# A matmul with a decaying cumulative sum: the second quarter of w as float32 by SyncE's queue

## The chip, the cores and the metric

The kernel runs on one core of a Trainium2 chip. The metric is the device time of one execution in microseconds (us). Three runs of the kernel before gave 904.08, 904.32 and 904.46 us, median 904.32. Engines are called as in the profile: PE (TensorE, matmuls), PEld (its weight loads), DVE (VectorE), ACT (ScalarE), POOL (GpSimd) and SP (SyncE, which only issues transfers).

## The reference

```python
B, S, D = (16, 2048, 1024)      # x [B,S,D], w [D,D], decay [D], all float32

def reference(x, w, decay):
    xw = x @ w
    out[:, 0, :] = xw[:, 0, :]
    for t in range(1, S):
        out[:, t, :] = decay * out[:, t - 1, :] + xw[:, t, :]
    return out
```

A matrix product, and along time a first-order recurrence for each of the 1024 output columns.

## The kernel before

Time is cut into 64 chunks of 512 steps (`chunks`, four for each of the 16 batches). The 1024 input columns are cut into four quadrants of 256, each on 32 partitions. x is loaded by POOL's queue and cast to bfloat16 on the way (`load`, line 105), turned in blocks of 32 by 32 on DVE (`turn`, line 115, tile `xw`), and copied apart into `xt` (`part`, line 123), the form in which the matmuls read it. In the first two chunks some matmuls read `xw` directly.

Eight matmuls, k = 0 to 7, sum over the input columns; k = 2m + e, with m the row set (0 to 3) and e the parity of the row of w. Eight output groups n = 0 to 7 of 128 columns belong to two halves h of w's columns. So w comes in four quarters (h, e), each of four row sets m. A quarter is loaded into `stage[h, e]`, which borrows room from output tiles (`room`), by four transfers, one for each quadrant (`load_w`, line 319). It is then settled into the weight tile `wsb`, row set by row set, by a copy on DVE or ACT that also makes it bfloat16 if it isn't (`settle`, line 326; `settle_slots`, line 375, does one row set in two pieces).

- Quarter (0,0) comes as float32, two transfers by SP's queue and two by ACT's, at the very start.
- Quarters (0,1), (1,0), (1,1) are issued by POOL, cast to bfloat16 during the transfer.

The first four output groups run together for the first two chunks (step 0 of the main loop): first all even k of chunk 0, in two half chunks (columns of time 0 to 255, then 256 to 511), then k = 1, 3, 5, 7 of chunk 0 for four groups each, then chunk 1. So quarter (0,0) and x's first half chunk are needed first, then the second half chunk, then quarter (0,1), row set after row set, then chunk 1. Quarters (1,0) and (1,1) are needed from the fifth output group on.

Nothing is scheduled by a planner: every instruction is kept in the order of the program on its engine, and `agenda` is a list of steps written out by hand, each a letter and a number. The entry -99 is the order of the start:

- `M0` to `M3`: loads of x's half chunks (chunk 0 first half, second half, chunk 1 first half, second half), four transfers each by POOL.
- `U0` to `U2`: `load_part`, the last three quarters of w by POOL.
- `w0 W1 w2 W3`: settle quarter (0,0); small `w` on ACT, `W` on DVE. `q4 w5 Q4 W6 W7` settle quarter (0,1): `q4` and `Q4` are row set 0 in two pieces on DVE, `w5` row set 1 on ACT, `W6` and `W7` row sets 2 and 3 on DVE. `W8` to `W11` and `w12` to `w15` settle the last two.
- `K0` to `K3`: `spin_on`, ACT copies one column of quadrant q of x's first half chunk into a gate tile, on which a few idle matmuls wait.
- `E0` to `E15`: turns on DVE, four for each half chunk; `F` and `G`: the copies into `xt` on DVE and ACT.
- `D`: the decay rows are turned, copied and squared on DVE.

POOL's queue holds eight transfers before an issue has to wait for the one eight places earlier to land.

After the start the kernel repeats: matmuls for two chunks and one output group, the recurrence on DVE and, for some tiles, in pairs with POOL and ACT, turning back on DVE, stores by SP's queue (`Outlet.store`, line 302).

Of the kernel before, what the change touches and what calls it, by code (L numbers as in the profile page):

```python
# [10 lines left out]
BF16 = mybir.dt.bfloat16  # L11
# [3 lines left out]
def _ap(ap_obj: bass.AP, new_ap, extra_offset=0):  # L15
    return dataclasses.replace(
        ap_obj,
        ap=[list(p) for p in new_ap],
        offset=ap_obj.offset + extra_offset,
    )  # L20
# [5 lines left out]
def kernel(  # L26
# [26 lines left out]
    nc = tc.nc  # L53
    pin = tc.keep_in_program_order
    B, S, D = x.shape
    assert w.shape == (D, D)

    NQ = 4
    P = 32
    CQ = D // NQ  # L60
    K = CQ // P
    M = K // 2
# [4 lines left out]
    CH = D // 2  # L67
# [8 lines left out]
    def ring(pool, name, count, shape, dtype=FP32):  # L76
        i = turns[name] = turns.get(name, -1) + 1
        return pool.tile(shape, dtype, name=f"{name}{i % count}")

    def quad(q):  # L80
        return slice(q * P, (q + 1) * P)
# [12 lines left out]
    def ot_tile(nj):  # L94
        return ring(sb, "ot", 4, [128, nj, CR])

    xb_of = {}
# [12 lines left out]
    def turn(c, j0=0, j1=NJ, m0=0, m1=M):  # L110
        if c not in xw_of:
            xw_of[c] = ring(sb, "xw", 2, [128, M, NJ, P, 2], BF16)
        src = xb_of[c][:, j0:j1].rearrange("p j c -> p (j c)").bitcast(FP32)
        dst = xw_of[c].rearrange("p m j i e -> p (m j i e)").bitcast(FP32)
        pin(nc.vector.transpose(  # L115
            out=dst.rearrange("p (m j i) -> p j m i", m=M, i=P)[:, j0:j1, m0:m1],
            in_=src.rearrange("p (j m c) -> p j m c", m=M, c=P)[:, :, m0:m1]))
# [168 lines left out]
    class Outlet:  # L286
# [8 lines left out]
        def store(self, b, t0):  # L295
# [4 lines left out]
            for j in range(0, self.nj, nj):  # L300
# [9 lines left out]
    room = [ot_tile(2 * NJ).rearrange("p j c -> p (j c)") for _ in range(2)]  # L310
    size = M * CH
    stage = {(0, 0): room[0][:, 0:size],
             (0, 1): room[0][:, size:size * 3 // 2].bitcast(BF16),
             (1, 0): room[1][:, 0:size // 2].bitcast(BF16),
             (1, 1): room[1][:, size // 2:size].bitcast(BF16)}

    def load_w(queues, h, e):
        for i, q in enumerate((0, 2, 1, 3)):
            pin(queues[i % len(queues)].dma_start(  # L319
                out=stage[h, e][quad(q)].rearrange("p (m d) -> p m d", m=M),  # L320
                in_=_ap(w, [[2 * D, P], [2 * P * D, M], [1, CH]],
                        (q * CQ + e) * D + h * CH)))
# [26 lines left out]
    for q in range(NQ):  # L349
        pin(nc.sync.dma_start(  # L350
            out=rows[q * P:q * P + R],
            in_=_ap(decay, [[P, R], [CH, 2], [1, P]], q * CR)))
# [8 lines left out]
        spin(3 if q < NQ - 1 else 2, gates[q])  # L361

    def load_part(i):
        load_w((nc.gpsimd,), *((0, 1), (1, 0), (1, 1))[i])

    def part_one(i, copy):
        part(i // 8, copy, i % 4, i % 4 + 1, *halves[i // 4 % 2])
# [105 lines left out]
    def turn_and_load(c):  # L473
# [16 lines left out]
        "w": lambda i: settle_one(i, nc.scalar.copy),  # L490
        "M": load_half,
        "U": load_part,
        "E": lambda i: turn(i // 8, *halves[i // 4 % 2], i % 4, i % 4 + 1),
        "F": lambda i: part_one(i, nc.vector.tensor_copy),
        "G": lambda i: part_one(i, nc.scalar.copy),
# [22 lines left out]
        "L": lambda i: load(*loads.pop(0)) if loads else None,  # L518
    }
    agenda = {  # L520
        -99: "M0 M1 U0 M2 M3 U1 U2 w0 W1 w2 W3 K0 K1 K2 K3 E0 E1 G0 E2 G1 E3 F2 G3 E4 E5 G4 E6 G5 E7 F6 G7 q4 w5 Q4 W6 W7 D E8 E9 G8 E10 G9 E11 F10 G11 E12 L E13 G12 L E14 G13 E15 L F14 G15",
        0: "p0 z0 W8 W9 W10 W11",
        1: "g0",
        2: "L S1 L",
# [199 lines left out]
```

## Time and profile before

| | |
|---|---|
| median of three runs | 904.32 us (904.08 to 904.46) |
| the profiled execution, its own time | 903.77 us |
| its span | 902.0 us |
| POOL's queue (q0): packets, MB, share of 16 engines | 137024, 68.70, 56.9% |
| SP's queue (q1): packets, MB, share of 16 engines | 265808, 134.77, 60.6% |
| w by POOL's queue | 12 transfers of 128 KB, 5.1 us median from issue to landing |
| w by SP's and ACT's queues | 2 + 2 transfers of 256 KB, 4.7 and 5.2 us |
| x half chunks | 16 transfers of 128 KB, 5.9 us |

The span runs from the first to the last recorded instruction; the execution's own time is a little longer. Sizes are those written into the core's memory: a quarter of w is 1 MB as float32 and 512 KB as bfloat16. Where a matmul or a copy sat idle, the timeline names in brackets for how long and what ended the wait. A wait for several transfers ends with the last of them.

### The profile page before, as it was taken

Reading aid. Unit: us, or ns where it says so; the run is one execution under the profiler, and the core shown is the slowest. Engines: PE = TensorE matmul, PEld = TensorE weight load, DVE = VectorE, ACT = ScalarE, POOL = GpSimd, SP = SyncE. Lnnn points to the kernel's source line nnn. Section 1 sums busy time; section 2 is a strip of 40 time slices with the busy share of each in tenths; the row PEclk is TensorE's granted clock in tenths of the full one; section 3 lists DMA queues with packets and bytes.
Section 4 is the critical chain, followed back from the end, with each engine's and each line's share of the span. In section 5 each row is a group of like instructions: output and inputs, shape, how many; then the busy total and the mean of one; then the engine's idle time right before and its main releaser. Section 6 shows DMA issues by size and latency. Waiting matters only on the chain.

```text
span 902.0 us, 12224 instructions
## 1 busy us (share of the span) xinstructions
PE 892.4 (99%) x4127; PEld 412.1 (46%) x4209; DVE 824.9 (91%) x635; ACT 687.6 (76%) x962; POOL 656.6 (73%) x755
## 2 busy tenths in 40 slices
PE   9999999999999999999999999999999999999998
PEld 5544444444444444444444444444444444444444
DVE  4999998999999999999998999999999999999998
ACT  4889967777877877878778778777787787787743
POOL 7888678777767778777677686777777777776532
PEclk9999999999999999999999999999999999999999
DMA  9999999999999999999999999999999999999858
GB/s 191 194 215 220 229 243 218 215 218 249 244 243 254 231 258 251 251 243 250 225 234 227 223 234 224 232 228 226 233 230 227 227 231 225 226 228 222 176 146 239
DMA packets 403182, 204.77 MB, mean 227 GB/s; under 512 B 9392, under 2 KB 402096, under 8 KB 403120
## 3 DMA queue, kind: packets, MB, share of 16 engines
q1 hardware_dynamic: 265808, 134.77, 60.6%
q0 software_dynamic: 137024, 68.70, 56.9%
q8 instruction: 33, 0.54, 0.2%
q10 hardware_dynamic: 288, 0.52, 0.2%
q14 instruction: 29, 0.24, 0.1%
HBM read 138.42 MB, written 134.22 MB: 302 GB/s over the span
## 4 chain that ended last, share of the span: by engine, by line
PE 97%; DMA 1%; issue 1%; POOL 0%; DVE 0%; ACT 0%; DVEq 0%; POOLq 0%
PE ps L131 96%; PE spare L131 1%; DMA xb<-in_x_dram 1%; DMA ot<-in_w_dram 1%; POOL ot L319 0%; DVE so L233 0%; POOL xb L105 0%; PE ps L415 0%; PE spare L415 0%; ACT xb L422 0%; DVE wsb L375 0%; DVEq L375 0%; POOLq L708 0%
## 5 line engine op out<-in xcount | busy, mean ns | idle before, releaser
L131 PE MATMUL ps<-xt,wsb 128*128 128x512 bf16 x3934 | 860.8, 378 | 4.5 <-DVE wsb L375 0.2
L131 PEld LDWEIGHTS <-wsb 128*128 128x128 bf16 x4160 | 406.7, 98 | 478.7 <-ACT wsb L326 0.8
L208 POOL TENSOR_TENSOR xs<-h,xs 128x512 f32<-128x512 f32 (+1 forms) x190 | 242.8, 1278 | 188.2 <-ACT h L169 85.0
L186 ACT COPY xs<-ps 128x1024 f32<-128x1024 f32 (+1 forms) x190 | 188.8, 994 | 153.6 <-PE ps L131 143.2
L278 DVE STREAM_TRANSPOSE ot<-so 128x1024 f32<-128x1024 f32 (+2 forms) x264 | 300.2, 1175 | 2.3 <-POOL so L202 1.1
L266 POOL TENSOR_TENSOR so<-h,xs 128x512 f32<-128x512 f32 (+1 forms) x190 | 241.1, 1271 | 42.6 <-ACT h L169 27.1
L123 ACT COPY xt<-xw 128x2048 bf16<-128x2048 bf16 (+1 forms) x136 | 242.3, 1790 | 7.8 <-DVE xw L115 7.8
L105 POOL DMA_DIRECT2D xb<-in_x_dram x264 | 173.9, 660 | 3.4 <-DMA ot<-in_w_dram 1.3
L169 ACT ACTIVATE h<-so,dec 128x512 f32<-128x512 f32 (+1 forms) x190 | 145.5, 766 | 27.8 <-DVE so L213 24.5
L115 DVE STREAM_TRANSPOSE xw<-xb 128x2048 f32<-128x2048 f32 (+1 forms) x78 | 147.3, 1901 | 6.7 <-DMA xb<-in_x_dram 6.7
L213 DVE TENSOR_TENSOR_SCAN so<-spare,keep,xs 128x512 f32<-128x512 f32 (+1 forms) x97 | 119.9, 1239 | 26.7 <-POOL xs L208 26.3
L213 DVE TENSOR_TENSOR_SCAN so<-spare,xs 128x512 f32<-128x512 f32 x93 | 113.3, 1220 | 27.2 <-POOL xs L208 24.4
L169 ACT ACTIVATE h<-ps,dec 128x512 f32<-128x512 f32 (+1 forms) x189 | 129.5, 685 | 0.0
L233 DVE TENSOR_TENSOR_SCAN so<-dec,ps 128x1024 f32<-128x1024 f32 x34 | 76.9, 2260 | 0.8 <-ACT h L169 0.6
L233 DVE TENSOR_TENSOR_SCAN so<-dec,keep,ps 128x1024 f32<-128x1024 f32 (+2 forms) x35 | 74.7, 2137 | 0.0
L270 ACT COPY keep<-so 128x1 f32<-128x1 f32 x136 | 25.2, 188 | 9.2 <-DVE so L233 8.7
L204 ACT COPY so<-keep 128x1 f32<-128x1 f32 x97 | 18.4, 191 | 2.5 <-DVE ot L278 2.3
L131 PE MATMUL spare<-xt,wsb 128*128 128x512 bf16 (+1 forms) x64 | 12.9, 332 | 0.0
L131 PE MATMUL ps<-xw,wsb 128*128 128x256 bf16 (+1 forms) x68 | 11.2, 301 | 0.0
L202 POOL MEMSET so<- 128x1 f32 x93 | 10.7, 117 | 0.6 <-DVE ot L278 0.6
L319 POOL DMA_DIRECT2D ot<-in_w_dram x12 | 6.5, 545 | 3.6 <-DMA xb<-in_x_dram 2.5
L344 PE MATMUL spare<-idle 128*128 128x512 bf16 x22 | 7.1, 499 | 1.2 <-DVE idle L334 1.2
(40 smaller groups left out, 40.5 us busy)
## 6 DMA issues: line engine op xcount, KB each, us to landing
out_dram<-ot SPq DMA_DIRECT2D x236, 512.0 KB, 11.1
xb<-in_x_dram POOLq DMA_DIRECT2D x248, 256.0 KB, 7.9
out_dram<-ot SPq DMA_DIRECT2D x56, 128.0 KB, 2.6
xb<-in_x_dram POOLq DMA_DIRECT2D x16, 128.0 KB, 5.9
out_dram<-ot SPq DMA_DIRECT2D x8, 256.0 KB, 4.5
ot<-in_w_dram POOLq DMA_DIRECT2D x12, 128.0 KB, 5.1
out_dram<-xb SPq DMA_DIRECT2D x4, 256.0 KB
ot<-in_w_dram ACTq DMA_DIRECT2D x2, 256.0 KB, 5.2
```

Source lines behind the costliest of these rows:

```text
L105: pin(nc.gpsimd.dma_start(out=xb_of[c][quad(q), j0:j1], in_=_ap(x, [[D, P], [P * D, j1 - j0], [1, CQ]], (b * S + t0 + j0 * P) * D + q * CQ)))
L115: pin(nc.vector.transpose(out=dst.rearrange("p (m j i) -> p j m i", m=M, i=P)[:, j0:j1, m0:m1], in_=src.rearrange("p (j m c) -> p j m c", ...
L123: pin(copy(out=xt_of[c][:, m0:m1, :, j0 * P:j1 * P], in_=src))
L131: pin(nc.tensor.matmul(out=ps[:, t0:t1] if ps.shape[1] >= t1 else ps, lhsT=lhs, rhs=rhs, start=(k == 0 and t0 == start), stop=(k == K - 1),))
L169: pin(nc.scalar.activation(out=h, in_=src, func=mybir.ActivationFunctionType.Copy, scale=dec[:, self.n:self.n + 1]))
L186: pin(nc.scalar.copy(out=self.xs[:, i * size:(i + 1) * size], in_=ps))
L208: pin(nc.gpsimd.tensor_tensor(out=odds, in0=self.g, in1=odds, op=ALU.add))
L213: pin(nc.vector.tensor_tensor_scan(out=so[:, 3:T + 2:2], data0=squares[-1][:, n:n + 1].to_broadcast([128, T // 2]), data1=self.xs[:, 1:T:2 ...
L233: pin(nc.vector.tensor_tensor_scan(out=so[:, t + 2:t + 2 + size], data0=dec[:, n:n + 1].to_broadcast([128, size]), data1=ps, initial=befor ...
L266: pin(nc.gpsimd.tensor_tensor(out=self.so[:, 2:T + 2:2], in0=self.h, in1=self.xs[:, 0:T:2], op=ALU.add))
L270: pin(nc.scalar.copy(out=self.keep, in_=self.so[:, self.T + 1:self.T + 2]))
L278: pin(nc.vector.transpose(out=outlet.ot[:, :, c0:c0 + P], in_=self.so[:, 2 + t0:2 + t0 + nj * P].rearrange("p (i t) -> p i t", t=P)))
```

## The change

The second quarter of w, (0,1), is no longer cast in the transfer. Its place in `stage` is twice as long and holds float32. `U0` is gone, and `load_part` now serves the last two quarters only. A new step `O` (`load_rows`) stands behind the gate copies K0 to K3: ACT copies one element of the last quadrant of x's first half chunk into the stage, and then SP issues eight transfers of 128 KB: row sets 0 and 1 of all four quadrants, then row sets 2 and 3. The first transfer overwrites the copied element and so waits for the copy; the other seven stand behind it in SP's queue.

```diff
     stage = {(0, 0): room[0][:, 0:size],
-             (0, 1): room[0][:, size:size * 3 // 2].bitcast(BF16),
+             (0, 1): room[0][:, size:2 * size],
              (1, 0): room[1][:, 0:size // 2].bitcast(BF16),
              (1, 1): room[1][:, size // 2:size].bitcast(BF16)}
...
     def load_part(i):
-        load_w((nc.gpsimd,), *((0, 1), (1, 0), (1, 1))[i])
+        load_w((nc.gpsimd,), 1, i - 1)
+
+    def load_rows(i):
+        pin(nc.scalar.copy(
+            out=stage[0, 1][quad(0), 0:1], in_=xb_of[0][quad(NQ - 1), 0, 0:1]))
+        for m in range(0, M, 2):
+            for q in range(NQ):
+                pin(nc.sync.dma_start(
+                    out=stage[0, 1][quad(q), m * CH:(m + 2) * CH].rearrange(
+                        "p (m d) -> p m d", m=2),
+                    in_=_ap(w, [[2 * D, P], [2 * P * D, 2], [1, CH]],
+                            (q * CQ + 2 * m * P + 1) * D)))
...
+        "O": load_rows,
...
-        -99: "M0 M1 U0 M2 M3 U1 U2 w0 W1 w2 W3 K0 K1 K2 K3 E0 E1 G0 E2 G1 E3 F2 G3 E4 E5 G4 E6 G5 E7 F6 G7 q4 w5 Q4 W6 W7 D E8 E9 G8 E10 G9 E11 F10 G11 E12 L E13 G12 L E14 G13 E15 L F14 G15",
+        -99: "M0 M1 M2 M3 U1 U2 w0 W1 w2 W3 K0 K1 K2 K3 O E0 E1 G0 E2 G1 E3 F2 G3 E4 E5 G4 E6 G5 E7 F6 G7 q4 w5 Q4 W6 W7 D E8 E9 G8 E10 G9 E11 F10 G11 E12 L E13 G12 L E14 G13 E15 L F14 G15",
...
```

The order of everything else, and the number of matmuls, turns and settling copies, is the same.

## The prediction

> **What bounds the kernel now.** I read the page first: busy shares, then the chain of work that ended last.
>
> ```profile
> PE 892.4 (99%) x4127; PEld 412.1 (46%) x4209; DVE 824.9 (91%) x635; ACT 687.6 (76%) x962; POOL 656.6 (73%) x755
> ...
> PE 97%; DMA 1%; issue 1%; POOL 0%; DVE 0%; ACT 0%; DVEq 0%; POOLq 0%
> ```
>
> TensorE is the bound and nothing else is near it: 97% of the chain is matmuls. The small rest is the start, so a change in how w arrives can only matter there. The stretches table gives PE 835.9 us busy of the 840 between 30 and 870 us, so a delay at the start is not made up later: each microsecond that the early matmuls lose is added to the end. So I read the timeline of the first 25 us (start, duration, engine, line, operation, count, and in brackets the idle time before it and what ended it):
>
> ```profile
> 7.32 1.14 ACT L326 CAST wsb<-ot 128x512 bf16<-128x512 f32 x2 [4.15 <-DMA ot<-in_w_dram]
> 7.36 0.76 DVE L326 CAST wsb<-ot 128x512 bf16<-128x512 f32 x2 [5.85 <-DMA ot<-in_w_dram]
> ...
> 9.88 0.19 ACT L360 COPY gate<-xb 32x1 bf16<-32x1 bf16 x1 [0.40 <-DMA xb<-in_x_dram]
> ...
> 10.40 1.66 ACT L123 COPY xt<-xw 128x512 bf16<-128x512 bf16 x3 [0.34 <-DVE xw L115]
> ...
> 12.50 1.42 DVE L115 STREAM_TRANSPOSE xw<-xb 128x256 f32<-128x256 f32 x4 [0.84 <-DMA xb<-in_x_dram]
> ...
> 14.88 0.36 DVE L375 COPY wsb<-ot 128x128 bf16<-128x128 bf16 x2 [0.66 <-DMA ot<-in_w_dram]
> ...
> 15.13 0.82 PE L131 MATMUL ps<-xt,wsb 128*128 128x512 bf16 x2 [0.17 <-DVE wsb L375]
> ...
> 16.87 0.81 PE L131 MATMUL ps<-xt,wsb 128*128 128x512 bf16 x3
> ...
> 17.62 1.42 DVE L115 STREAM_TRANSPOSE xw<-xb 128x256 f32<-128x256 f32 x4 [1.35 <-DMA xb<-in_x_dram]
> ...
> 18.60 0.84 PE L131 MATMUL ps<-xw,wsb 128*128 128x256 bf16 x6
> ```
>
> At 9.88 ScalarE sees the last quarter of x's first half chunk; at 12.50 VectorE has the second half chunk; at 14.88 the second quarter of w is in and the odd rows k=1 start at 15.13. The groups before them came every 0.45 us (13.90, 14.35), so k=1 could have started at 14.80: 0.33 us is all that an earlier second quarter can gain. From 15.13 on matmuls run without a gap: k=5 starts at 16.87, the second chunk at 18.60, 0.98 us after its first turn began at 17.62.
>
> **The change part by part.** *Removed:* the four GpSimd issues of the second quarter (0.54 us each). GpSimd's other issues move up four places: M2, M3, U1 and U2 each take the slot and the landing waits that the four before them had, so M2 is issued from 8.21 to about 10.8 where the second quarter was. No transfer of x needed before 12.50 is behind them. Nothing on the path is saved by the issuing itself.
>
> *Added on ScalarE:* one 1-column copy behind the last gate copy. The four such copies take 0.19 us each; the last ends at 10.07 and the next instruction waits for VectorE until 10.40, so it fits into the 0.34 us of idle time: cost 0. Without that cover it would put 0.19 us on the turned x.
>
> *Added on SyncE:* eight issues that start when that copy ends, 10.26. SyncE issued two 256 KB transfers in 0.86 us, so eight take some 3.2 us, ending at 13.5. Queued behind them are only the output stores, the first at 38.94: free. From the first issue at 0.75 to flowing data (the stretches show DMA share 0.01 in 1 to 2 us, 0.79 in 2 to 3) went 1.1 to 1.25 us; so data flow from about 11.4.
>
> *Moved onto the path: how fast 1 MB of float32 comes while GpSimd's queue is full of x.* The DMA view of three stretches (9 to 11, 2 to 5.4, and 50 to 60 us) has the rates:
>
> ```profile
> q0 software_dynamic: 801, 0.39, 144.6%
> ```
> ```profile
> DMA packets 504, 0.95 MB, mean 278 GB/s; under 512 B 42, under 2 KB 42, under 8 KB 504
> ```
> ```profile
> q0 software_dynamic: 2144, 1.07, 77.1%
> q1 hardware_dynamic: 2145, 1.08, 52.7%
> ```
>
> GpSimd's queue alone sends 801 packets in 2 us; 46 of them are under 512 B, which leaves 378 data packets (512 B) per us. The hardware queues alone sent 462 packets of 2 KB in 3.4 us, 136 per us. When both are loaded they send equal numbers, 214 and 214 per us: packet for packet. The second quarter is now 512 packets of 2 KB. Alternating, they take 512/136 + 512/378 = 3.76 + 1.35 = 5.1 us and so end at 16.5; the first half (two row sets of all quadrants) after 2.55 us, at 13.95. A landing is seen later than its last packet: x's second half chunk is the last of 8 transfers whose packets end near 11.7 and is seen at 12.50; for the first quarter of w it was about 1 us. I take 0.9. First half seen at 14.85, the same as now (14.88); second half at 17.4.
>
> *What the second half holds up.* VectorE settles row set 2 (W6) from float32: 0.42 us by the mean of the two CAST rows (0.32 is its mean for all bfloat16 copies; ScalarE's 0.62 does not differ). So k=5 starts at 17.4 + 0.42 + 0.15 = 18.0 instead of 16.87: **+1.1 us**. W7 is ready 0.4 later, k=7 is wanted 0.86 later: hidden. The float32 column copies q4, Q4 cost at most 0.15 more, but k=1 late by that much is inside the later wait for k=5. So is a delay of x's second half chunk: its last packets (to 11.7) meet the new ones for 0.3 us, at most 0.4 us more, and k=5 would still be wanted by 17.3.
>
> *What is late next.* On VectorE's queue W6, W7, the three decay instructions (15.64 to 16.27, 0.63 us) and then the turn E8 of the second chunk stand in order: 17.4 + 0.84 + 0.63 = 18.9. Its data: of M2's 1024 packets 512 went between the others, 512 remain: 16.5 + 1.35 + 0.7 = 18.55. A turned block was used 0.49 us after its turn began (12.50 to 12.99): 19.4, wanted at 18.0 + 1.73 = 19.7. Covered, by 0.3 us only. M3 (20.31 now) comes about 1.1 later, as matmuls do; U1 and U2 stay behind them and move likewise, with over 1 us between the first settle of U1 (24.25) and its use (25.72).
>
> *Bounds for the one term not in the trace.* Below: if the new packets lose nothing to x, 1.05 MB at 278 GB/s take 3.8 us; the second half is seen at 16.1, k=5 is on time and k=1 can start at 14.80: -0.33. Above: if both queues together move only the 193 GB/s that GpSimd's alone shows, 1.05 + 0.26 MB take 6.8 us, 1.7 more: +2.8. I take +1.1, because two queues together moved 215 GB/s over the 50 to 60 us stretch with writes of 512 B (1.07 + 1.08 MB), and 254 GB/s (the rows of 4 to 6 us) give 5.2 us.
>
> **Sum.** -0 (issues) +0 (gate copy) +1.1 (k=5) +0 (the rest) on 903.77 for the profiled execution (span 902.0). The median shown is 904.32, 0.55 more; on it: 904.3 + 1.1 = **905.4**.
>
> **The rivals.**
> *Hidden anyway (0.15).* The float32 stream gets most of the bandwidth and the second half is in before 16.3. For it: 2 KB packets carry four times the bytes of x's at equal count. Against it: that is already counted. Time: 904.0 to 904.6, so 904.2.
>
> *The second chunk takes over (0.20).* The two streams slow each other, towards 193 GB/s, or E8, behind W7 and the decay instructions, passes its 0.3 us of cover; a second half seen after 18.1 makes it cost over 1.8 us. For it: a small margin, and 2 KB rows read beside x. Against it: the rates add up well in 50 to 60 us. +1.9 to +2.8: about 906.7.
>
> *Runs instead of single packets (0.10), the slower side.* An engine might send one transfer's whole share before it turns to the other queue. Shared among the page's 16 DMA engines, a new transfer (64 packets) has 4 on each, M2's (256) has 16: a round is 4 x 16/136 + 16 x 16/378 = 0.47 + 0.68 = 1.15 us, eight rounds 9.2 us. The second half would be seen at 11.4 + 9.2 + 0.9 = 21.5, k=5 at 22.0: +5.1, **909.4**. It costs over 1.8 us from about six packets of x to four new ones (rounds of 0.73 us). Against it: in 50 to 60 us a store of 512 KB has twice the packets of an x transfer, and whole shares would give 2 to 1, not 2145 to 2144; equal but long runs, cut short by small transfers, would not show there.
> [...]
>
> *The gate doesn't hold (0.02).* If the eight transfers went out behind the decay rows (3.07), x's first half chunk would be late by some 2.5 us: 906.8. Against it: the built program's first of them waits for ScalarE.
>
> **How the numbers follow.** My forecast's chance is 0.53, with 904.7 to 906.1 of its own. 0.2% is 1.8 us, about what a measurement of this kernel can tell from no change. Hidden (0.15) and forecast (0.53) lie within it; the second chunk, runs and gate (0.32) are slower. No row offers more than 0.33 us of gain, so 0.02 for faster is what I may have overlooked, taken from the middle: 0.66. The range 904.1 to 907.4 leaves out the runs and little else.
>
> **What would show it.** Right: k=1 near 15.1 as before; a gap of about 1.1 us on PE before k=5, ended by VectorE's settle that waits for w; equal packet counts of q0 and q1 from 11.5 to 16.5; the second chunk 19.6 to 19.8. Wrong: no gap (hidden), a gap before the second chunk ended by its turn, or q0 far ahead of q1 in packets (runs).

## The result and the profile after

The changed kernel takes 909.23 us (median of 6 runs, 908.62 to 909.79) where the kernel before takes 904.19 us beside it (6 runs, 903.72 to 904.46): a ratio of 1.0056, 95% interval 1.0043 to 1.0069, 5.0 us slower. The prediction was 905.4 us with a range of 904.1 to 907.4, so it was wrong: the direction was right, the size was not.

From the page of the changed kernel, the busy shares and the chain that ended last:

```profile
span 907.5 us, 12230 instructions
...
PE 893.7 (98%) x4127; PEld 412.3 (45%) x4209; DVE 825.5 (91%) x635; ACT 687.5 (76%) x963; POOL 655.1 (72%) x751
...
PE 97%; DMA 2%; issue 1%; SPq 0%; POOL 0%; DVE 0%; ACT 0%; DVEq 0%; ACTq 0%; POOLq 0%
```

TensorE still does the same 4127 matmuls, and the span is 5.5 us longer than the 902.0 before. TensorE's busy time grew by 1.3 us only; the rest is idle time. The chain has twice the share of DMA, and SyncE's sequencer (SPq) is new in it. The timeline of the start, against the lines shown in the prediction:

```profile
10.00 0.19 ACT L360 COPY gate<-xb 32x1 bf16<-32x1 bf16 x1 [0.46 <-DMA xb<-in_x_dram]
...
10.21 0.19 ACT L367 CAST ot<-xb 32x1 f32<-32x1 bf16 x1
10.43 4.34 SPq L371 DMA_DIRECT2D ot<-in_w_dram  x8
...
12.54 1.43 DVE L115 STREAM_TRANSPOSE xw<-xb 128x256 f32<-128x256 f32 x4 [0.77 <-DMA xb<-in_x_dram]
...
18.49 0.50 DVE L386 CAST wsb<-ot 128x128 bf16<-128x128 f32 x2 [4.21 <-DMA ot<-in_w_dram]
...
18.77 0.44 PE L131 MATMUL ps<-xt,wsb 128*128 128x512 bf16 x1 [3.76 <-DVE wsb L386]
...
21.85 0.76 DVE L326 CAST wsb<-ot 128x512 bf16<-128x512 f32 x2 [2.86 <-DMA ot<-in_w_dram]
...
22.34 0.83 PE L131 MATMUL ps<-xt,wsb 128*128 128x512 bf16 x3
...
24.09 0.84 PE L131 MATMUL ps<-xw,wsb 128*128 128x256 bf16 x6
```

Up to 12.54 all is as before, within 0.15 us: x's first chunk is not disturbed. Then w is late twice. The first half is seen at 18.49 (before: 14.88), and TensorE idles 3.76 us ahead of k=1. The second half is seen at 21.85, and k=5 starts at 22.34 instead of 16.87, 5.47 us late. The second chunk follows 1.75 us later, as before (1.73), and nothing changes after that: 5.47 us at k=5 are the 5.5 us of the span. Three further traces with the same eight transfers (the kernel again, and twice with the idle time filled, as told below) agree: k=5 starts at 21.13, 20.69 and 21.87, so 4.3, 3.8 and 5.0 us late, and their spans of 906.3, 905.8 and 907.0 us are longer by just that. The late start of k=5 is the whole loss.

The stretches of the same trace show one more thing (us; then for each engine its busy time and, in brackets, its instructions; then granted clock, DMA share, GB/s):

```profile
17.00:19.00 2.00, 0.23 (x1) 0.10 (x1) 0.50 (x2) 0.53 (x1) 1.05 (x2) 1.00 1.24 231
19.00:21.00 2.00, 1.77 (x5) 0.73 (x6) 0.00 (x0) 0.09 (x1) 0.43 (x2) 0.50 1.41 196
21.00:23.00 2.00, 1.88 (x6) 0.47 (x5) 1.09 (x4) 0.00 (x0) 0.92 (x3) 0.65 1.26 203
```

Behind the idle time TensorE's granted clock is 0.50 from 19 to 21 us: five matmuls fill 2 us, where nine would at the 0.22 us each of k=5 (four from 22.34 to 23.22).

### The profile page after: what moved, and what is told of

The parts are those of the page before. It is cut to its first block, busy times and chain, and to the rows that moved or that the text cites. A ratio compares the mean times of both kernels' runs of the same rounds, so it can differ in the third digit from the quotient of the medians.

```text
span 907.5 us, 12230 instructions
## 1 busy us (share of the span) xinstructions
PE 893.7 (98%) x4127; PEld 412.3 (45%) x4209; DVE 825.5 (91%) x635; ACT 687.5 (76%) x963; POOL 655.1 (72%) x751
## 4 chain that ended last, share of the span: by engine, by line
PE 97%; DMA 2%; issue 1%; SPq 0%; POOL 0%; DVE 0%; ACT 0%; DVEq 0%; ACTq 0%; POOLq 0%
PE ps L131 95%; PE spare L131 1%; DMA ot<-in_w_dram 1%; DMA xb<-in_x_dram 1%; SPq L371 0%; POOL xb L105 0%; DVE so L233 0%; PE ps L426 0%; DVE wsb L326 0%; PE spare L426 0%; ACT xb L433 0%; ACT ot L367 0%; ACT gate L360 0%; DVEq L326 0%; ACTq L360 0%
## 5 line engine op out<-in xcount | busy, mean ns | idle before, releaser
L204 ACT COPY so<-keep 128x1 f32<-128x1 f32 x97 | 18.4, 191 | 2.4 <-DVE ot L278 2.2
L131 PE MATMUL ps<-xw,wsb 128*128 128x256 bf16 (+1 forms) x68 | 11.2, 301 | 0.0
L319 POOL DMA_DIRECT2D ot<-in_w_dram x8 | 4.5, 567 | 5.6 <-DMA xb<-in_x_dram 5.4
## 6 DMA issues: line engine op xcount, KB each, us to landing
out_dram<-ot SPq DMA_DIRECT2D x236, 512.0 KB, 10.5
```

The costliest lines, as they stand in the source:

```text
L131: pin(nc.tensor.matmul(out=ps[:, t0:t1] if ps.shape[1] >= t1 else ps, lhsT=lhs, rhs=rhs, start=(k == 0 and t0 == start), stop=(k == K - 1),))
```

## The experiments

Times are medians; "before" is the kernel before, measured beside each group of runs, whose medians differ by up to 0.7 us. "First packet", "last packet" and the time between are read from the trace's packet records, for the 512 packets of 2 KB that carry the second quarter. A row's trace is of one execution: for the pause behind M2 it took 906.08 us, for float32 by GpSimd 907.43, both well off their medians, and the text says what that means.

In these kernels "quiet" keeps x's packets away until all of w's second quarter has landed, "x held" and "pause" keep back some of them, "idle time filled" adds matmuls on zeros where TensorE waited, and "float32 by GpSimd" drops the cast without using a second queue.

| kernel | us | before | ratio, 95% interval | first packet | last packet | between |
|---|---|---|---|---|---|---|
| changed | 909.23 | 904.19 | 1.0056 [1.0043, 1.0069] | 12.95 | 20.39 | 7.4 |
| the same again | 908.79 | 903.96 | 1.0053 [1.0038, 1.0068] | 12.85 | 19.32 | 6.5 |
| idle time filled | 907.61 | 903.46 | 1.0046 [1.0030, 1.0062] | 13.05 | 18.98 | 5.9 |
| the same again | 908.18 | 903.96 | 1.0047 [1.0032, 1.0062] | 13.04 | 20.10 | 7.1 |
| quiet | 911.72 | 903.99 | one run | 10.97 | 15.68 | 4.7 |
| four transfers | 910.70 | 903.99 | one run | 12.89 | 18.23 | 5.3 |
| the same again | 911.30 | 903.96 | 1.0079 [1.0063, 1.0094] | 12.89 | 18.68 | 5.8 |
| four, idle time filled | 909.12 | 904.05 | 1.0057 [1.0037, 1.0077] | 12.66 | 18.46 | 5.8 |
| sixteen transfers | 912.78 | 903.99 | one run | 13.05 | 23.09 | 10.0 |
| two queues | 908.64 | 903.99 | one run | 12.59 | 18.70 | 6.1 |
| x held for half of w | 908.74 | 904.05 | 1.0057 [1.0042, 1.0072] | 11.23 | 15.93 | 4.7 |
| no gate | 909.86 | 904.05 | 1.0068 [1.0053, 1.0083] | 8.50 | 16.00 | 7.5 |
| pause behind M2 | 907.42 | 903.46 | 1.0044 [1.0029, 1.0059] | 12.86 | 17.97 | 5.1 |
| x held ahead of M2 | 906.21 | 903.46 | 1.0025 [1.0014, 1.0037] | 11.10 | 17.71 | 6.6 |
| float32 by GpSimd | 906.08 | 904.05 | 1.0027 [1.0016, 1.0039] | | | |
| the same, idle time filled | 905.90 | 903.96 | 1.0023 [1.0013, 1.0032] | | | |

### Is it x's packets, or SyncE's queue by itself? The quiet kernel

```diff
+    held = const.tile([128, 1], FP32, name="held")
+
+    def hold(i):
+        pin(nc.gpsimd.tensor_copy(out=held, in_=stage[0, 1][:, size - 1:size]))
...
+        "H": hold,
```

The start's order becomes `M0 M1 w0 W1 w2 W3 K0 K1 K2 K3 O H M2 M3 U1 U2`, then as before.

> GpSimd issues nothing more for x or w until the last of the eight float32 transfers has landed (a one-column copy on GpSimd reads it first), so from x's second half chunk on they have the engines to themselves. Turns (an engine gives each queue a run of packets, and the four that a new transfer puts on an engine make a short run; the loss comes from x's packets between): alone they flow at the 136 packets per us of the first quarter, data from 11.6 to 15.5, row sets 2 and 3 settled from about 16.5, k=1 on time near 15. Supply (SyncE's queue is fed late and slowly by itself, first packet 2.5 us after the issue and 0.77 us for each transfer, whatever else runs): data from 12.9 to 19, row sets 2 and 3 settled from about 20.3, k=1 late by 2 us or more. Under both the second chunk is late, since x is held back, so the total tells nothing.

Its timeline:

```profile
10.02 3.60 SPq L371 DMA_DIRECT2D ot<-in_w_dram  x8
...
14.58 0.49 DVE L391 CAST wsb<-ot 128x128 bf16<-128x128 f32 x2 [0.38 <-DMA ot<-in_w_dram]
...
16.50 0.76 DVE L326 CAST wsb<-ot 128x512 bf16<-128x512 f32 x2 [1.42 <-DMA ot<-in_w_dram]
...
16.98 0.82 PE L131 MATMUL ps<-xt,wsb 128*128 128x512 bf16 x3 [0.16 <-DVE wsb L326]
```

Row sets 2 and 3 are seen at 16.50, as forecast for x's packets being the cause, and k=5 is on time (16.98, before 16.87). That the time fits to the tenth is luck: the first packet came 0.6 us earlier than forecast (10.97, not 11.6) and the 512 took 4.7 us, not 3.9. A slow or late SyncE by itself falls: the same eight transfers, issued 10.02, have their first packet 0.95 us later and take 4.7 us. Their issue, behind the gate from 10.02, is not too late either. What x's packets do to them is what is left to explain.

### Where the late start comes from: two pauses of GpSimd

The held copy reads x's second half chunk instead (`xb_of[0][:, NJ - 1, CQ - 1:CQ]`). In one kernel it stands behind M2 (`M0 M1 M2 H M3 ...`), in the other ahead of it (`M0 M1 H M2 M3 ...`).

> The changed kernel, but GpSimd waits between its four issues of M2 and its four of M3 until x's second half chunk has landed (a one-column copy on GpSimd reads it), so that it issues nothing from 10.8 to 12.5, while M2 stands in its queue as before. It tells two reasons for the late first packet (12.94, 2.5 us after SyncE's issue) apart. GpSimd's issuing keeps SyncE's packets back: first packet near 11.4, both halves 1.5 us earlier, total near 907.5. Packets of x that the engines have already taken in go first (some 60 on each, 2.5 us): M2 alone is as many, first packet near 12.9 as before, total within 1 us of the changed kernel's.

> The changed kernel, but GpSimd waits ahead of M2, not behind it, until x's second half chunk has landed: when SyncE's transfers are issued, only the rest of the first chunk stands in GpSimd's queue. Packets already taken in go first: the first new packet comes when x's second half chunk ends, near 11, as in the quiet kernel; M2's packets come from about 13.5, when some 270 of the 512 are through. First half seen near 14.8, k=1 on time; the other 240 share with x at 80 per us, to 16.6, seen near 17.8, k=5 near 18.4, 1.5 us late; x's second chunk seen near 18.5: total 905.5 to 906.5, 3 us better than the changed kernel. If the first packet is late for a reason of SyncE's own: 908 or more.

The DMA view of 11.0 to 12.8 us, for the changed kernel, the pause behind M2 and the hold ahead of it, in this order (packets, MB, share of 16 engines):

```profile
q0 software_dynamic: 700, 0.34, 142.5%
```
```profile
q0 software_dynamic: 726, 0.35, 145.6%
```
```profile
q1 hardware_dynamic: 239, 0.40, 67.2%
q0 software_dynamic: 107, 0.05, 19.9%
```

In the first two SyncE's queue (q1) is absent, though its transfers were issued from 10.43 and 9.91. GpSimd issued nothing between 10.3 and 12.8 in the second, so its issuing is not what keeps them back. In the third only the end of x's first chunk stood in GpSimd's queue, and 239 packets (completion records among them) are through. So in these runs the new packets waited for most of the packets of x that stood before them: first packets at 12.6 to 13.05 in every gated kernel with M2 in the queue, at 11.0 to 11.2 in each without. In the changed kernel that is 2.5 us behind the issue instead of 0.95, by my estimate some 59 packets of x on each engine (2.5 us at the 378 per us of the prediction, over 16 engines). The packet records of the traces say it more closely. When the first new packet came, x had sent 10.3 to 10.8 transfers' worth of packets in the ten traces with the gate and M2 in the queue, of the 11 or 12 transfers issued ahead of it, and 7.7 to 7.8 of 8 in the three without M2. Where the packets are held (in the engine or ahead of it) no run shows.

The kernel before has the same wait with the queues exchanged, at its very start:

```profile
0.75 0.86 SPq L319 DMA_DIRECT2D ot<-in_w_dram  x2
...
1.33 4.71 POOL L105 DMA_DIRECT2D xb<-in_x_dram  x8 [0.88 <-POOLq L708]
```

The first packet of x is at 5.49, 4.2 us behind its issue, when 476 of the 512 packets of w's first quarter (SyncE's and ScalarE's, issued first) had been sent. With no other packets ahead, in the quiet kernel, x's second chunk was issued at 17.01 and began at 18.30, 1.3 us behind.

The total of the pause was forecast within 1 us of the changed kernel's, and missed on the good side: 907.4, where the changed kernel took 908.8 and 909.2. In the trace M2's packets ran out, since M3 was held back, and the 512 took 5.1 us. But that trace is of the fastest of its four runs (906.08 us, with a mean granted clock of 0.999); the other three took 907.25 to 907.67 us at 0.998, so with a stretch of slow TensorE clock in them (see the section on the slow clock). The hold ahead of M2 came as forecast in its total, 906.2 us (904.85 to 906.63 in seven runs), with k=1 at 14.94 and k=5 at 18.80 (forecast 18.4):

```profile
18.80 0.82 PE L131 MATMUL ps<-xt,wsb 128*128 128x512 bf16 x3 [1.91 <-DVE wsb L326]
```

But x's second chunk was turned only at 20.79 (forecast seen near 18.5), and TensorE waited 0.59 us more for it, so that here part of the loss is x's. It is the best of all variants with SyncE's transfers, and still slower than the kernel before, by 2.7 us in the medians and 2.3 by the ratio.

### What sets the pace: four, eight and sixteen transfers, and two queues

```diff
-        for m in range(0, M, 2):
-            for q in range(NQ):
...
+        for q in range(NQ):
+            pin(nc.sync.dma_start(
+                out=stage[0, 1][quad(q)].rearrange("p (m d) -> p m d", m=M),
+                in_=_ap(w, [[2 * D, P], [2 * P * D, M], [1, CH]],
+                        (q * CQ + 1) * D)))
```

Sixteen transfers take one row set of one quadrant each, in the same way. For two queues, `nc.sync` becomes `(nc.sync, nc.scalar)[q % 2]`.

> The same data in four transfers of 256 KB (all row sets of a quadrant), so each puts 8 packets of 2 KB on an engine instead of 4. Turns by a transfer's share: rounds of 8 new to some 10 of x (0.94 + 0.42 = 1.36 us), four of them, 5.5 us instead of the 7.7 us of the changed kernel (12.92 to 20.60): all row sets seen near 19.7, k=5 2 us earlier than in the changed kernel, total about 907. Supply by issue (0.54 us for each): half the issues, as fast or faster. Turns that end after a fixed number of packets or of time, whatever the transfer: the same 7.7 us, all row sets near 21.8; k=1 is then as late as k=5, total about 2 us above the changed kernel's.

> The same data in sixteen transfers of 64 KB, row set by row set, 2 packets on an engine each. Turns by a transfer's share: sixteen rounds of 0.24 + 0.42 = 0.66 us, 10.5 us instead of 7.7: the last row set is seen near 24.7, total 3 us above the changed kernel's. Supply by issue: 16 x 0.54 = 8.6 us of issuing from 10.4, the last packets about 2.5 later, 21.5, near the changed kernel's 20.6. Turns of a fixed size in packets or time: no change, 20.6.

> Quadrants 0 and 2 by SyncE's queue, 1 and 3 by ScalarE's, the same eight transfers in the same order. Turns between queues, of whatever size: the new packets get two turns for each of x, so the data take 5.5 us or less instead of 7.7, second half seen near 19.7, and x's second chunk is slower by as much. Supply: two queues feed twice as fast, about 4 us, second half near 18.2, first half near 16. A limit of the engines' bandwidth, shared by bytes or time: 7.7 us as before. ScalarE's four issues put up to 2 us on its copies of x, which k=1 needs only at 15.

The DMA view of 14 to 16 us, for the changed kernel, four, sixteen, and two queues:

```profile
q0 software_dynamic: 455, 0.22, 82.0%
q1 hardware_dynamic: 190, 0.32, 47.5%
```
```profile
q1 hardware_dynamic: 204, 0.38, 78.4%
q0 software_dynamic: 237, 0.11, 43.6%
```
```profile
q0 software_dynamic: 514, 0.25, 92.2%
q1 hardware_dynamic: 186, 0.26, 41.6%
```
```profile
q10 hardware_dynamic: 126, 0.21, 43.9%
q1 hardware_dynamic: 122, 0.21, 43.0%
q0 software_dynamic: 169, 0.08, 31.0%
```

With four large transfers the two queues went nearly packet for packet (237 of x to 204), with eight it was 2.4 of x to one new, with sixteen 2.8 (completion records are among the counts). Two hardware queues got 248 to x's 169. The whole 512 packets take 5.3 and 5.8 us by four transfers, 10.0 by sixteen, as the theory of turns by a transfer's share had it (5.5 and 10.5).

The total of four was forecast at 907 and came out at 910.7: with four transfers k=1, too, waits for all of w, which the forecast left out, and the slow clock behind that wait (below) adds to it. Two queues were forecast at 5.5 us or less and took 6.1, within what eight transfers by one queue show below, so that a gain from the second hardware queue is not shown.

The middle of the range of sizes is not that firm either. The eight were run again beside the four on one chip:

> The changed kernel once more, unaltered, for a second trace beside the next ones on one chip. In its first trace the 512 packets took 7.4 us, in the kernel with matmuls on zeros, whose transfers are the same, 5.9 us. If turns by a transfer's share set the pace: 7 to 7.5 us again. If the pace varies from run to run: anything from 5.9 up, and a share of 4 or 8 packets to an engine makes no certain difference.

> Four transfers of 256 KB once more (5.3 us for the 512 packets the first time). Turns by share: 5.3 to 5.8, two us below the changed kernel in the same call. Pace that varies: the two overlap. In either case k=1 waits for all row sets, the clock falls to half, and the total is 1 to 1.5 us above the changed kernel's.

The eight took 6.5 us this time, the four 5.8; the total of the four is 2.5 us above that of the eight, not the 1 to 1.5 of the forecast. Over four traces with the same eight transfers the pace is 5.9, 6.5, 7.1 and 7.4 us, over three with four transfers 5.3, 5.8 and 5.8. The ranges come within 0.1 us of each other, so that the size of a transfer counts between four and eight is likely and not shown. Sixteen lie outside, but there SyncE's last eight issues also wait for earlier transfers to land (eight waits, 4.7 us in all, the ninth issue at 14.33 behind the eighth at 12.97), so its 10.0 us are not share alone. What is shown: alone 4.7 us, beside x 5.3 to 7.4, and in the changed kernel x gets 1.1 (17 to 19 us: 232 to 211) to 2.4 packets for each new one.

### The slow clock

To the kernel of four transfers 21 matmuls on zeros are added; the changed kernel gets 16 in the same place, the kernel with float32 by GpSimd 10.

```diff
+            for _ in range(21):
+                pin(nc.tensor.matmul(
+                    out=spares[1], lhsT=idle[:, 0:128], rhs=idle, start=True, stop=True))
             for k in range(1, K, 2):
```

> The kernel of four 256 KB transfers, with 21 matmuls on zeros into a bank that is not yet used, put between the first chunk's even and odd k, where TensorE sat idle for 4.9 us. It adds work that the output does not need. In the kernel of four the granted clock was 0.50 from 21 to 23 us, behind that idle time, and eight matmuls took 0.43 us each instead of 0.22: if idle time causes it and it costs on the path, 8 x 0.21 = 1.7 us come back, total about 909 instead of 910.7. If the slow matmuls only fill a wait for something else: no change.

> The changed kernel with 16 matmuls on zeros in the place where TensorE sat idle for 3.8 us (work that the output does not need). The slow clock behind the idle time (0.50 from 19 to 21 us) falls on k=1 and k=3, and k=5 waits for row set 2 until 22.2 anyway: no change, within 0.6 us of 909.2. If the slow clock is on the path here as in the kernel of four: 1.6 us less, 907.6.

> The changed kernel with 16 matmuls on zeros once more, now beside the changed kernel on the same chip. Slow clock only beside a wait for row set 2: the same time as the changed kernel within 0.5 us. Slow clock on the path: 1 to 1.6 us less.

TensorE's timeline of the kernel of four transfers, and of the same with its idle time filled:

```profile
19.55 1.30 PE L131 MATMUL ps<-xt,wsb 128*128 128x512 bf16 x3 [4.86 <-DVE wsb L384]
...
21.07 1.49 PE L131 MATMUL ps<-xt,wsb 128*128 128x512 bf16 x3
```
```profile
14.56 4.48 PE L645 MATMUL spare<-idle 128*128 128x512 bf16 x20
...
19.91 0.88 PE L131 MATMUL ps<-xt,wsb 128*128 128x512 bf16 x3 [0.88 <-DVE wsb L384]
...
20.84 0.81 PE L131 MATMUL ps<-xt,wsb 128*128 128x512 bf16 x3
```

From k=1 to k=3 takes 1.52 us (19.55 to 21.07, start to start) behind idle time and 0.93 (19.91 to 20.84) without; the total falls from 910.7 to 909.1 as forecast. There all of w has landed when k=1 starts, so each slow matmul counts. In the changed kernel the filling was expected to change nothing, since k=5 waits for row set 2 anyway. Beside each other on one chip: 908.79 without and 908.18 with it, intervals of the ratios that overlap. The first pair, 909.2 and 907.6, was not measured side by side and had its packets in 7.4 and 5.9 us, so it does not show the clock.

The mean granted clock of each run helps here. Of the ten runs of the changed kernel three have 1.000, so no slow stretch (0.50 for 3.4 us, from 19.0 to 22.4, in the trace, which alone makes the mean 0.998; a slow stretch at the very end of the span takes at most 0.001 of it in any trace), and took 908.45, 908.81 and 909.20 us; the other seven (0.996 to 0.998) took 908.04 to 909.79. So nearly all of the 5.0 us is there without the slow clock; by the medians, 908.8 and 909.3, it adds some half a microsecond, which is less than the runs differ by anyway. In the trace the slow matmuls end at 22.21 and row set 2 is in `wsb` for k=5 at 22.34, so the one hides behind the other.

### Holding x back, and no gate

In one kernel the held copy reads row set 1 (`stage[0, 1][:, 2 * CH - 1:2 * CH]`), order as in the quiet kernel. In the other the ScalarE copy at the head of `load_rows` is taken out.

> As the quiet kernel, but GpSimd goes on to x's second chunk as soon as the first four float32 transfers have landed, so that its packets arrive when the other four are nearly through. Turns: no packets of x between, so k=1 near 15 and k=5 near 17 as in the quiet kernel; x's second chunk is issued from 15 and flows from 15.7 to 18.5, its turn starts near 19.3 and its matmuls near 19.8 instead of 18.60: total 1.0 to 1.5 us above before, 905 to 905.6, and nearly 4 us better than the changed kernel with the same bytes in the same eight transfers. If instead float32 by SyncE's queue is slow whatever stands beside it: 908 or more.

> Without ScalarE's copy ahead of them the eight transfers are issued as soon as SyncE may reuse its semaphores, when the first quarter of w lands, near 6, the last four near 8. Turns, with a start that waits behind packets of x already taken in (2.5 us, as in the changed kernel): new data from about 8.5 to 16, all of it between x's first chunk; the second half chunk is complete near 15 instead of 11.7, its matmuls start near 16 instead of 13, k=1 near 18: total 3 to 3.5 us above before, about 907.5, better than the changed kernel. If the order of arrival is all that counts (row sets earlier is better, x's first chunk not slowed): k=1 and k=5 on time and a total within 1 us of before.

The first missed: w was in time (k=1 at 15.07, k=5 at 17.42), but x's second chunk, issued from 15.31, sent its first packet at 16.59 (forecast 15.7) and was turned at 21.55 instead of 19.3, and the matmuls, at 22.05, then ran at half clock (0.50 granted from 23 to 25 us). What w gains x loses. Without the gate x's second half chunk was held up as described, but for longer. The transfers are issued from 4.88, the last four from 7.82 (forecast near 6 and near 8), the new packets begin at 8.50, x's second half chunk is turned at 17.16 (before: 12.50) and its matmuls start at 17.66 (forecast near 16); TensorE idles 4.87 us ahead of them and goes to half clock (0.50 from 19 to 21 us): 909.9, not 907.5. So the gate in the changed kernel protects x's first chunk, as its place suggests, and gains nothing that can be told from the changed kernel's 1.0056.

### Float32 alone, without a second queue

```diff
-             (0, 1): room[0][:, size:size * 3 // 2].bitcast(BF16),
+             (0, 1): room[0][:, size:2 * size],
```

This is the only edit to the kernel before: GpSimd's queue, the old place, no cast.

> The kernel before with one part of the change alone: the second quarter as float32, still by GpSimd's queue at its old place (512 packets of 2 KB instead of 1 KB, no cast), settled from float32. Turns: no other queue is loaded, so only the larger packets cost: at 136 per us 3.8 us instead of 2.6, 1.2 us on k=1 and on everything behind it in the queue: 905.2 to 905.6. If float32 itself is what costs 5 us: about 909.

> The kernel before with the second quarter as float32 by GpSimd's queue (906.1 without the addition), and 10 matmuls on zeros (work that the output does not need) where TensorE sat idle for 2.3 us. If its 2.0 us are bytes (1.2 us) and a slow clock behind the idle time (the rest): 905.2 to 905.5. If all of it is late data: 906 as without.

906.08 and 905.90: float32 alone costs 2.0 us, not 1.2, and filling the idle time changes the median by less than the intervals tell, so the 2.0 us are late data and not clock.

But the clock shows here run by run. Five of the seven runs without the filling have a mean granted clock of 0.999 or 1.000 and took 905.84 to 906.38 us; the two at 0.997 took 907.43 and 908.01. With the idle time filled all ten are at 0.999 or 1.000 and the slowest took 906.72. So where TensorE's clock fell behind this wait of about 2.3 us, it cost 1 to 2 us more, and it fell in two runs of seven. The trace is of one of these two. From its timeline:

```profile
16.78 0.50 DVE L375 CAST wsb<-ot 128x128 bf16<-128x128 f32 x2 [2.91 <-DMA ot<-in_w_dram]
```

The quarter is seen at 16.78 instead of 14.88 (at 16.99 with the idle time filled). Its DMA view of 12 to 14 us has 137 packets for 0.46 MB, so they were sent in 4 KB pieces at 229 GB/s: 1.05 MB take 4.6 us at that rate, against 2.7 us for 0.52 MB at the 193 GB/s of the cast.

## Why the prediction was wrong

The step that failed is "Moved onto the path: how fast 1 MB of float32 comes while GpSimd's queue is full of x". Its three numbers, against the profiled execution of the changed kernel:

- "data flow from about 11.4": the first packet came at 12.95, **1.5 us** later. The 1.1 to 1.25 us were read at 0.75 us, when no packet of x stood in any queue. The quiet kernel and the hold ahead of M2 show 0.95 and 1.0 us where only the end of x's first chunk stood there; the pause behind M2, where M2 stood in GpSimd's queue, has 2.95 (9.91 to 12.86), so M2's packets make the difference.
- "5.1 us": 7.4 in this trace (5.9 to 7.4 in four), **2.3 us** more. One for one held nearly for four large transfers (5.3 to 5.8 us), and for the stores it was read from; beside eight small ones x sent up to 2.4 packets for one. Why the pace then differs from run to run is open.
- "I take 0.9" for the landing: 20.39 to 21.85, **0.5 us** more.

Together 4.3 us: k=5 at 22.34 instead of 18.0. The upper bound of the range was set for the pace alone (6.8 us instead of 5.1); none was set for the start or the landing. A start under load was in the trace before, twice: x's first packet 4.2 us behind its issue, as shown above, and the first store, issued at 38.94 with x in the queue, whose first packet is at 42.74, 3.8 us later.

The shortest starts of these transfers are 0.94 to 1.0 us (the quiet kernel, the two holds); the 2.5 us with M2 in the queue are far from them.

The rest of the working held:

- The gate copy cost nothing (ScalarE's next copy at 10.52, 0.11 behind it); x's first chunk was untouched; row set 2's settling took 0.44 us of the chain (0.42).
- What is late next was covered: VectorE turned the second chunk directly behind the decay instructions (23.18), and TensorE did not wait for it.
- Nothing made up for the delay after 30 us, and nothing was added: 5.47 us at k=5, 5.5 in the span.
- SyncE's issues took 4.34 us, not 3.2 (3.60 in the quiet kernel); the last was out at 14.77, 5.6 us ahead of the last packet, so this miss cost nothing that shows.

Of the rivals, runs of packets forecast 909.4 us, and the time came out there. The mechanism did not: its rounds (four new packets to sixteen of x, 9.2 us) are slower than any of the four traces (5.9 to 7.4), its start was the 11.4 of the forecast, and in 17 to 19 us the queues went 232 to 211. That its sum comes so near is luck: a start 1.5 us too early and a landing 0.5 us too short made up for a pace 1.8 us too slow. Its tenth was too little for what it stood for, though: that x sends more than one packet for each new one (1.1 to 2.4 in the changed kernel). The other rivals fell: nothing was hidden, the second chunk did not take over, the gate held.

The clock was missing from the prediction altogether. The traces show it: 0.50 granted behind 3.76 us of idle time in the changed kernel, for 3.4 us (19.0 to 22.4), and behind 4.86 and 5.09 us with four transfers. It also fell behind 2.31 us (float32 by GpSimd, 0.50 from 17 to 19 us) and did not behind 2.16 (pause behind M2, 1.00 in every stretch from 13 to 25 us). It does not fall in every run either: by the mean clocks, in two runs of seven of float32 by GpSimd. The length of one wait does not tell it here: with sixteen transfers the matmuls behind 2.27 us took 0.24 us each, and those behind 1.68 us more, soon after, 0.42. Where the clock fell, the slow matmuls added 1 to 2 us here if nothing else was late, by the runs of float32 by GpSimd and by the kernel of four (910.7 and 911.3 without the filling, 909.1 with it); the price of such a wait should hold them. In the changed kernel, where row set 2 was late as well, leaving it out cost the prediction some half a microsecond.

So of the 5.0 us, 2.0 are for float32 in the place of bfloat16, by the kernel that changes this alone. The other 3, by subtraction, are for the second queue beside x; no kernel takes that part alone, but holding x back ahead of M2 returns 2.3 to 2.7 us.

## What to carry to other kernels

The transfers that were moved to another queue did not escape the first one: with M2 in GpSimd's queue their first packet came 2.5 us behind the issue in the changed kernel, in the quiet kernel 0.95, and their 512 packets took 5.9 to 7.4 us instead of 4.7. So read a moved transfer's start and its pace from a place in the trace where both queues are loaded, with as much standing in the other one. A cast in the transfer that halves what is written was worth 2.0 us here, and without it just as many copies were needed. Behind stalls of 2.3 to 5.1 us on TensorE matmuls ran at a granted clock of 0.50 here, and not in every run of a kernel: look at the granted clock of each run before a single trace is taken for the median.

## What the runs showed that was not expected

- The first packet of a hardware-queue transfer came 0.95 us behind its issue with the other queue nearly empty and 2.5 to 3.3 us behind it with M2 standing there too, whether SyncE or ScalarE issued it (3.6 us without the gate). GpSimd's first x transfer waited 4.2 us in the same way behind packets of w.
- The pace of the same eight transfers beside the same x packets was 5.9, 6.5, 7.1 and 7.4 us in four traces, a spread of 1.5 us in one stage, while the totals of the kernel before lie within 1.2 us (903.3 to 904.5) in all measurements.
- Granted clock 0.50 for 3.4 us (the changed kernel) to 6.8 us (the second trace of four transfers, 17 to 25 us) behind 2.3 to 5.1 us of idle TensorE; with float32 by GpSimd in two runs of seven.
- The uncast float32 of GpSimd's queue went in 4 KB packets, 229 GB/s written, and cost 2.0 us.
